# Output projection of a hybrid encoder layer: four full products per 512 columns, or seven quarter products per 1024 columns with weight sums made by accumulating transfers

## The chip, the cores and the metric

One core of one Trainium2 chip runs the kernel. The metric is the device time of one execution in microseconds; several executions give a median. The engines are TensorE (PE; its weight loads are shown as PEld), VectorE (DVE), ScalarE (ACT), GpSimd (POOL) and SyncE (SP, which here only issues transfers). Sixteen DMA engines move data between DRAM and SBUF. The profile is one execution recorded by the hardware profiler.

## The reference

One layer over 16 meta tokens and 512 frames of width 2048, in float32. Only the end touches the change: `mix` (tokens x 2048) times `w_out` (2048 x 2048), added to the residual, then a final RMSNorm.

```python
hn = _rmsnorm(h_res, norm_in_g[l])
P = hn @ w_in[l]
...
y_a = (yn + bonus.reshape(bsz, L, D_RWKV)) * jax.nn.silu(g_r)
...
y_b = Bg * _causal_depthwise_conv(Cg * hc, conv_w[l]) * jax.nn.silu(g_c)
mix = jnp.concatenate([y_a, y_b], axis=-1)
h_res = h_res + mix @ w_out[l]
...
out = _rmsnorm(h_res, norm_f_g)
return out[:, N_META:]
```

## The kernel before

The kernel has two large matrix products and a recurrence between them. The input product (`steps`, L315) runs 65 column tiles of `w_in` through TensorE; it is a generator, and `fill` draws matmuls from it to put between the small matmuls of the recurrence (`recur`). TensorE's order is written by hand. On the other engines a scheduler sets the order, by what it expects to be ready; each engine then runs strictly in that order and waits at its next instruction. `ahead()` and `high_priority` move instructions forward in it.

Every float32 operand of a large product is split in two parts: `hi`, a rounded copy made by ACT, and `lo`, the rest, made by a subtraction on VectorE or POOL. A product is then three matmuls: hi x hi, hi x lo, lo x hi. `split_w` (L123) does it for a 128x512 quarter of weights; `hi` and `lo` have six buffers each. `prefetch` (L130) loads 128x1024 blocks (512 KB) through SP into three `raw` buffers and splits them. SP, too, runs in order: a load waits there until the `raw` buffer that it writes has been split.

`split_mix` (L1022) makes the left operand of the output product: for each of 16 tiles `j` of 128 mix columns (8 of the recurrence, 8 of the convolution) it loads the tile from DRAM, applies group-norm gain, bonus and gate where `j < 8`, and splits it. The last convolution tile (`cv7`) is written to DRAM (`mixd`) after the last input product and read back.

The output product (L1151 and following) goes over four blocks `n` of 512 output columns, 16 tiles `jj` of the contraction and four tiles `t` of 128 tokens; `accumulate` (L1080) issues the three matmuls. Each block uses four PSUM banks. `residual` (L1091) adds the bank to the residual rows `xr`, and takes the squares on ACT and the gain on POOL. The last block is split: its last six tiles `jj` run token tile by token tile (`load_last`, `last`), and the last token tile in two parts of 256 columns, so that norm, scaling and stores of the other rows (`finish`) overlap the rest. `row_part`, `row_scale` and `finish_last` make the norm of the last row and its four stores.

Of the kernel before, what the change touches and what calls it, by code (L numbers as in the profile page):

```python
# [76 lines left out]
def hymba_kernel(ctx: ExitStack, tc: tile.TileContext, xt, xtok, w_in, w_out, pv, lup, cst, msk, gf, out):  # L77
# [39 lines left out]
    for n in range(4):  # L117
        for g in range(8):
            stream.append(w_out[n, g])
# [897 lines left out]

    pp = ctx.enter_context(tc.tile_pool(name="pp", bufs=1, side="right", reuse_waits="tile"))
    order = list(range(KT))
    parts = {}  # L1020

    def split_mix(j):  # L1022
        parts[j] = [pp.tile([P, SEQ], F32R, name=f"m{a}{j}") for a in range(2)]
        mh, ml = parts[j]
        raw = pp.tile([P, SEQ], F32, tag="mraw", name=f"mr{j}", bufs=4)
        if j < NPAIR:
            rb = pp.tile([P, SEQ], F32, tag="rb", name=f"rb{j}", bufs=3)
            gg = pp.tile([P, SEQ], F32, tag="gg", name=f"gg{j}", bufs=3)
# [12 lines left out]
        nc.scalar.copy(mh, raw)  # L1041
        nc.vector.tensor_tensor(out=ml, in0=raw, in1=mh.bitcast(F32), op=ALU.subtract)
# [5 lines left out]
    for j in range(NPAIR):  # L1048
        split_mix(j)
        fill(FW["mix"])  # L1050
    for j in range(NPAIR + 4, KT):
        while ("gc", j - NPAIR) not in ready:
            step()
        run_pending(float("inf"))
        split_mix(j)
    for _ in flow:
        pass
    ph1.close()
# [4 lines left out]
    xr = [pw.tile([P, DM], F32, name=f"xres{t}") for t in range(4)]  # L1063
    gfb = pw.tile([P, DM], F32, name="gfb")
    ssq = pw.tile([P, 4, 5], F32, name="ssq")
    fv = pw.tile([P, 4, 3], F32, name="fv")
    NL = 6
    last = [[pw.tile([P, 512], F32R, name=f"wlast{a}{j}") for j in range(NL)] for a in range(2)]

    def load_last(jj):  # L1070
        j = N_IN + 3 * 8 + jj // 2
        if jj % 2 == 0:
            state["raw"] = wp.tile([P, 1024], F32, tag="raw", name=f"wr{j}", bufs=3)
            nc.sync.dma_start(state["raw"], stream[j])
        rq = state["raw"][:, (jj % 2) * 512 : (jj % 2 + 1) * 512]
        hi, lo = last[0][jj - (KT - NL)], last[1][jj - (KT - NL)]
        nc.scalar.copy(hi, rq)
        nc.vector.tensor_tensor(out=lo, in0=rq, in1=hi.bitcast(F32), op=ALU.subtract)

    def accumulate(ps, t, jj, hi, lo, parts_of=range(2)):  # L1080
        mh, ml = parts[order[jj]]
        tk = slice(t * P, (t + 1) * P)
        for q, (mm, ww) in enumerate(((mh, hi), (mh, lo), (ml, hi))):
            whole = len(ps) == 4 or t < 3
            for p in (0,) if whole else parts_of:
                o = slice(0, 512) if whole else slice(256 * p, 256 * p + 256)
                nc.tensor.matmul(  # L1087
                    ps[t + p], mm[:, tk], ww[:, o], start=(jj == 0 and q == 0), stop=(jj == KT - 1 and q == 2)
                )

    def residual(ps, n, t, part=None):  # L1091
        o = slice(0, 512) if part is None else slice(256 * part, 256 * part + 256)
        h = xr[t][:, n * 512 : (n + 1) * 512][:, o]
        nc.vector.tensor_tensor(out=h, in0=ps[t + (part or 0)], in1=h, op=ALU.add)
        sq = pw.tile([P, 512], F32, tag="sqj", name=f"sqj{n}_{t}_{part}", bufs=2)
        j = n + (part or 0)
        nc.scalar.activation(sq[:, o], h, AF.Square, scale=DM**-0.5, accum_out=ssq[:, t, j : j + 1])
        if n < 3:
            nc.gpsimd.tensor_tensor(out=h, in0=h, in1=gfb[:, n * 512 : (n + 1) * 512], op=ALU.mult)
        elif part is not None:  # L1100
            nc.vector.tensor_tensor(out=h, in0=h, in1=gfb[:, n * 512 : (n + 1) * 512][:, o], op=ALU.mult)

    scales = {}
# [6 lines left out]

    def row_scale(t, n):
        f = fv[:, t]
        w, u, r = f[:, 0:1], f[:, 1:2], f[:, 2:3]
        nc.gpsimd.tensor_scalar(out=u, in0=ssq[:, t, n : n + 1], scalar1=w, scalar2=None, op0=ALU.add)
        rsqrt(r, u)
        scales[t] = r

    def finish(t):
        r = scales[t]
        x = xr[t]  # L1120
        o = out[t * P : (t + 1) * P]
        nc.vector.scalar_tensor_tensor(
            out=x[:, 1536:DM], in0=x[:, 1536:DM], scalar=r, in1=gfb[:, 1536:DM], op0=ALU.mult, op1=ALU.mult
        )
        nc.gpsimd.tensor_scalar(
            out=x[:, 1024:1536], in0=x[:, 1024:1536], scalar1=r, scalar2=1.0, op0=ALU.mult, op1=ALU.mult
        )
        nc.scalar.activation(x[:, 0:1024], x[:, 0:1024], AF.Copy, scale=r)
        for a, b in ((1024, DM), (0, 1024)):
            nc.sync.dma_start(o[:, a:b], x[:, a:b])  # L1130

    def finish_last(t):
        r = scales[t]
        x = xr[t]
        o = out[t * P : (t + 1) * P]
        nc.vector.tensor_scalar(
            out=x[:, 1536:DM], in0=x[:, 1536:DM], scalar1=r, scalar2=1.0, op0=ALU.mult, op1=ALU.mult
        )
        nc.sync.dma_start(o[:, 1536:DM], x[:, 1536:DM])
        nc.scalar.activation(x[:, 0:512], x[:, 0:512], AF.Copy, scale=r)  # L1140
        nc.scalar.dma_start(o[:, 0:512], x[:, 0:512])
        nc.gpsimd.tensor_scalar(
            out=x[:, 1024:1536], in0=x[:, 1024:1536], scalar1=r, scalar2=1.0, op0=ALU.mult, op1=ALU.mult
        )
        nc.vector.tensor_scalar(
            out=x[:, 512:1024], in0=x[:, 512:1024], scalar1=r, scalar2=1.0, op0=ALU.mult, op1=ALU.mult
        )
        nc.sync.dma_start(o[:, 512:1024], x[:, 512:1024])
        nc.scalar.dma_start(o[:, 1024:1536], x[:, 1024:1536])

    for n in range(4):  # L1151

        ps = [
            po.tile([P, 512 if n < 3 or t < 3 else 256], F32, tag="o", name=f"o{n}_{t}") for t in range(4 if n < 3 else 5)
        ]
        first = KT if n < 3 else KT - NL
        for jj in range(first):
            idx = N_IN + n * 8 + jj // 2
            if jj % 2 == 0:
                prefetch(min(idx + 2, len(stream) - NL // 2))  # L1160
            if n < 2 and jj % 4 == 2:
                t, cols = jj // 4, slice(0, 512) if n == 0 else slice(512, DM)
                nc.sync.dma_start(xr[t][:, cols], xtok[t * P : (t + 1) * P, cols])
            if n == 0 and jj == KT - 1:
                nc.sync.dma_start(gfb, gf.partition_broadcast(P))
            if n == 3 and jj >= first - NL:
                load_last(jj + NL)
            hi, lo = quarters[2 * idx + jj % 2]
            for t in range(4):
                accumulate(ps, t, jj, hi, lo)  # L1170
        if n < 3:
            for t in range(4):
                residual(ps, n, t)
    with tc.manual_schedule(engines={mybir.EngineType.DVE, mybir.EngineType.Activation, mybir.EngineType.Pool}):
        for t in range(3):
# [4 lines left out]
            if t:  # L1180
                finish(t - 1)
# [70 lines left out]
```

## Time and profile before

| what | us |
|---|---|
| median of 3 runs (1049.66 to 1050.91) | 1050.04 |
| the profiled run | 1049.89 |
| span of the profiled execution | 1048.1 |
| mean granted TensorE clock | 0.996 of full |

The work of the last stage, in windows of the same execution (busy us of each engine in 20 us):

| window, us | PE | DVE | ACT | POOL | DMA share | GB/s |
|---|---|---|---|---|---|---|
| 870 to 890 | 20.00 | 3.34 | 4.97 | 4.42 | 0.82 | 300 |
| 890 to 910 | 20.00 | 5.35 | 6.81 | 7.85 | 0.28 | 79 |
| 910 to 930 | 20.00 | 2.08 | 4.35 | 7.39 | 0.35 | 106 |
| 970 to 990 | 20.00 | 2.77 | 4.69 | 3.88 | 0.36 | 106 |
| 990 to 1010 | 20.00 | 9.68 | 8.98 | 9.82 | 0.35 | 106 |

Busy time is the time in which an engine had an instruction running; a matmul's record overlaps the next one's, so a full PE column says that TensorE never waited, not that it was at its peak. The DMA share is the mean busy share of the 16 DMA engines. "Wait" and "releaser" in the profile are inferred from semaphores.

### The profile page before, as it was taken

How to read it: one execution, taken by the hardware profiler on the slowest of the kernel's cores; microseconds unless marked ns; L12 is line 12 of the kernel's file. 1: busy time of each engine (PE TensorE's matmuls, PEld its weight loads, DVE VectorE, ACT ScalarE, POOL GpSimd, SP SyncE). 2: the span in 40 equal slices, each digit the busy share in tenths (PEclk: the TensorE clock that was granted, in tenths of full speed). 3: DMA queues.
4: the chain of work that ended last, by engine and by line, in shares of the span. 5: the costliest groups of instructions: out<-in, count | busy, mean ns of one | idle time of the engine just before them, and what ended most of it. 6: DMA issues, size and time to landing. Idle time of an engine off the chain costs nothing.

```text
span 1048.1 us, 23743 instructions
## 1 busy us (share of the span) xinstructions
PE 1030.6 (98%) x9845; PEld 940.2 (90%) x9845; DVE 577.1 (55%) x1088; ACT 359.7 (34%) x666; POOL 302.2 (29%) x315
## 2 busy tenths in 40 slices
PE   8999999999999999999999999999999999999996
PEld 6999997999988999989999989889898988888885
DVE  6787865569653768643767642344554781212222
ACT  7554322534322433222433222222222432323232
POOL 0132323323232322222323221233323132424132
PEclk9999999999999999999999999999999999999998
DMA  8437385374854274754374748677655978332324
GB/s 292 142 103 175 84 215 143 99 176 102 213 143 118 84 187 105 182 157 116 104 171 115 186 127 291 232 222 241 186 152 137 270 214 304 101 87 94 101 61 161
DMA packets 183404, 167.48 MB, mean 160 GB/s; under 512 B 121472, under 2 KB 143744, under 8 KB 182912
## 3 DMA queue, kind: packets, MB, share of 16 engines
q1 hardware_dynamic: 182720, 164.90, 55.6%
q8 instruction: 77, 1.26, 0.5%
q10 hardware_dynamic: 576, 1.07, 0.3%
q14 instruction: 31, 0.25, 0.1%
HBM read 129.05 MB, written 36.88 MB: 158 GB/s over the span
## 4 chain that ended last, share of the span: by engine, by line
PE 92%; DMA 4%; DVE 2%; SPq 1%; issue 1%; ACT 0%; POOL 0%; DVEq 0%; ACTq 0%
PE o L1087 17%; PE ps_v L315 9%; PE ps_gc L315 9%; PE ps_k L315 9%; PE ps_g L315 9%; PE ps_r L315 8%; PE ps_B L315 8%; PE ps_C L315 7%; PE ps_h L315 7%; PE g L631 2%; PE zs L954 1%; PE ps_lora L315 1%; PE zy L958 1%; DMA gated<-g 1%; PE rz L902 1%; DVE wl L127 1%
## 5 line engine op out<-in xcount | busy, mean ns | idle before, releaser
L127 POOL TENSOR_TENSOR wl<-wr,wh 128x512 fp32r<-128x512 f32 x150 | 204.4, 1363 | 466.0 <-ACT wh L126 450.4
L126 ACT CAST wh<-wr 128x512 fp32r<-128x512 f32 x312 | 189.7, 618 | 407.1 <-PE o L1087 93.9
L127 DVE TENSOR_TENSOR wl<-wr,wh 128x512 fp32r<-128x512 f32 x162 | 122.2, 761 | 205.9 <-ACT wh L126 204.7
L1087 PE MATMUL o<-wh,m 128*128 128x512 f32 (+1 forms) x484 | 145.4, 384 | 0.0
L1087 PEld LDWEIGHTS o<-wh,m 128*128 128x128 f32 x484 | 89.6, 188 | 21.3
L1087 PE MATMUL o<-wl,m 128*128 128x512 f32 (+1 forms) x242 | 92.7, 390 | 0.0
L315 PE MATMUL ps_v<-xh,wh 128*128 128x264 f32 x256 | 73.2, 286 | 0.0
L315 PE MATMUL ps_h<-xh,wh 128*128 128x258 f32 (+1 forms) x256 | 73.0, 285 | 0.0
L315 PE MATMUL ps_k<-xh,wl 128*128 128x264 f32 x256 | 73.0, 285 | 0.0
L315 PE MATMUL ps_k<-xh,wh 128*128 128x264 f32 x256 | 73.0, 285 | 0.0
L315 PE MATMUL ps_v<-xh,wl 128*128 128x264 f32 x256 | 72.8, 284 | 0.0
L315 PE MATMUL ps_v<-xl,wh 128*128 128x264 f32 x256 | 72.8, 284 | 0.0
L315 PE MATMUL ps_k<-xl,wh 128*128 128x264 f32 x256 | 72.7, 284 | 0.0
L315 PE MATMUL ps_C<-xh,wh 128*128 128x258 f32 (+1 forms) x256 | 72.7, 284 | 0.0
L315 PE MATMUL ps_r<-xh,wh 128*128 128x258 f32 (+1 forms) x256 | 72.3, 282 | 0.3 <-ACT wh L225 0.3
L315 PE MATMUL ps_g<-xl,wh 128*128 128x258 f32 (+1 forms) x256 | 72.5, 283 | 0.0
L315 PE MATMUL ps_h<-xl,wh 128*128 128x258 f32 (+1 forms) x256 | 72.1, 281 | 0.3 <-issue 0.3
L315 PE MATMUL ps_h<-xh,wl 128*128 128x258 f32 (+1 forms) x256 | 72.3, 282 | 0.0
L315 PE MATMUL ps_r<-xh,wl 128*128 128x258 f32 (+1 forms) x256 | 72.1, 282 | 0.0
L315 PE MATMUL ps_r<-xl,wh 128*128 128x258 f32 (+1 forms) x256 | 72.1, 282 | 0.0
L315 PE MATMUL ps_C<-xl,wh 128*128 128x258 f32 (+1 forms) x256 | 72.1, 282 | 0.0
L315 PE MATMUL ps_g<-xh,wh 128*128 128x258 f32 (+1 forms) x256 | 72.1, 281 | 0.0
(274 smaller groups left out, 2705.2 us busy)
## 6 DMA issues: line engine op xcount, KB each, us to landing
wr<-in_w_in_dram SPq DMA_DIRECT2D x127, 512.0 KB
ct<-opd SPq DMA_DIRECT2D x64, 288.0 KB
wr<-in_w_out_dram SPq DMA_DIRECT2D x32, 512.0 KB
opd<-ar SPq DMA_DIRECT2D x8, 576.0 KB
opd<-gt SPq DMA_DIRECT2D x16, 288.0 KB
opd<-bt SPq DMA_DIRECT2D x64, 64.0 KB
xres<-in_xtok_dram SPq DMA_DIRECT2D x4, 768.0 KB
out_dram<-xres SPq DMA_DIRECT2D x6, 512.0 KB
```

Source lines behind the costliest of these rows:

```text
L126: nc.scalar.copy(hi, rq)
L127: eng.tensor_tensor(out=lo, in0=rq, in1=hi.bitcast(F32), op=ALU.subtract)
L315: nc.tensor.matmul(ps[r], ww[:, w], xx[:, kt, a:b], start=(kt == 0 and n == 0), stop=(kt == KT - 1 and n == 2))
L631: nc.tensor.matmul(z[h][:, c - c0], bk[hs, c, h : h + 2, :].rearrange("p a s -> p (a s)"), ar[hs, c].rearrange("p a s -> p (a s)"), start= ...
L902: nc.tensor.matmul(z[e][ho if e else hs, 0, k], t[hs, o : o + CH], t[hs, O_V : O_V + CH] if part else st[hs, 4 * e + k], start=(part == 0 ...
L954: nc.tensor.matmul(d[hs, j], w, x[hs], start=(a == 0), stop=(a == b - 1))
L958: nc.tensor.matmul(d[ho, j], t[hs, o : o + CH], x[hs], start=(a == 0), stop=(a == b - 1))
L1087: nc.tensor.matmul(ps[t + p], mm[:, tk], ww[:, o], start=(jj == 0 and q == 0), stop=(jj == KT - 1 and q == 2))
```

## The change

The input side stays as it is. The output product is done for 1024 output columns at a time ("half"). For each half the matrices are cut in quarters, `A` (tokens x contraction) by token half and contraction half, `B` (contraction x columns) likewise, and the four quarters of the result come from seven products of quarters (Strassen's method in Winograd's form) in place of eight. A product is four "units" `g`; a unit is one 512 KB block of weights, two tiles of the contraction, two tiles of tokens, twelve matmuls. The order of products is M1, M2, M7, Q6, P5, P4, M3.

The left sums (`S3`, `S5`, `S1`, `S4`) are made by VectorE in place in `mix` (`sums`), and split into hi and lo by `split_form`. The right sums are made by transfers: SP loads a block of `B`, then POOL issues a transfer that adds another block to it in SBUF (`add`); for Q6 and P4 the block of the product before is added to again (`chain`). Each unit is split two units ahead (`split_unit`), now always with the subtraction on VectorE. `close` combines a finished product into the residual rows `here(t, n)` and a shared sum. The table `calls` says at which unit each load, add and split is written in the program; the scheduler orders the engines but TensorE as before. The weights of the last product of the second half are loaded and split early (`load_home`) into buffers of forms no longer used. Rows are finished in the order 2, 3, 0, 1.

```diff
-    for n in range(4):
-        for g in range(8):
-            stream.append(w_out[n, g])
+    stream += [w_out[0, g] for g in range(2)]
...
+    mix = [pp.tile([P, 4, SEQ], F32, tag=f"R{m}", name=f"mix{m}") for m in range(4)]
...
-        nc.scalar.copy(mh, raw)
-        nc.vector.tensor_tensor(out=ml, in0=raw, in1=mh.bitcast(F32), op=ALU.subtract)
+        nc.scalar.copy(mh, raw[:, 0:n])
+        nc.vector.tensor_tensor(out=ml, in0=raw[:, 0:n], in1=mh.bitcast(F32), op=ALU.subtract)
...
+    forms = {"S3": (0, T1), "S5": (0, T0), "S1": (2, T1), "S4": (2, T0)}
+    def quarter(k, tk, q):
+        return mix[2 * k + q][:, :, tk]
+    def sums(q):
+        a11, a21, a12, a22 = quarter(0, T0, q), quarter(0, T1, q), quarter(1, T0, q), quarter(1, T1, q)
+        nc.vector.tensor_tensor(out=a22, in0=a22, in1=a21, op=ALU.subtract)
+        nc.vector.tensor_tensor(out=a21, in0=a11, in1=a21, op=ALU.subtract)
+        nc.vector.scalar_tensor_tensor(out=a11, in0=a22, scalar=-1.0, in1=a11, op0=ALU.mult, op1=ALU.subtract)
+        nc.vector.scalar_tensor_tensor(out=a12, in0=a11, scalar=-1.0, in1=a12, op0=ALU.mult, op1=ALU.subtract)
...
+    sums(0)
...
+    sums(1)
...
+    def split_form(f, q):
+        k, tk = forms[f]
+        x = mix[k + q][:, :, tk]
+        hi, lo = sform[f, q]
+        nc.scalar.copy(hi, x)
+        nc.vector.tensor_tensor(out=lo, in0=x, in1=hi.bitcast(F32), op=ALU.subtract)
+    PRODUCTS = ("M1", "M2", "M7", "Q6", "P5", "P4", "M3")
+    LEFT = {"M1": 0, "M2": T0, "M7": "S3", "Q6": "S5", "P5": "S1", "P4": T1, "M3": "S4"}
+    units = [(half, prod, g) for half in range(2) for prod in PRODUCTS for g in range(4)]
...
+    def request(u):
+        half, prod, g = units[u]
+        if prod in ("M1", "M2", "M3"):
+            k, c = {"M1": (0, 0), "M2": (1, 0), "M3": (1, 1)}[prod]
+        elif prod == "M7":
+            slot[u] = chain[g] = pw.tile([P, 1024], F32, tag=f"X{g}", name=f"x{half}{g}")
+            nc.sync.dma_start(slot[u], rows_of(half, 0, 1, g))
+            return
+        elif prod == "P5":
+            k, c = 0, 0
+            if g < 2:
+                slot[u] = spare[0][:, 1024 * g : 1024 * g + 1024]
+                nc.sync.dma_start(slot[u], rows_of(half, k, c, g))
+                return
+        else:
+            slot[u] = chain[g]
+            return
+        slot[u] = wp.tile([P, 1024], F32, tag="raw", name=f"wo{u}", bufs=3)
+        nc.sync.dma_start(slot[u], rows_of(half, k, c, g))
+    ADDED = {"M7": (1, 1), "Q6": (0, 0), "P5": (0, 1), "P4": (1, 0)}
+    def add(u):
+        half, prod, g = units[u]
+        if prod in ADDED:
+            k, c = ADDED[prod]
+            nc.gpsimd.dma_start(slot[u], rows_of(half, k, c, g), accum_op=ALU.add)
+    def split_unit(u, home=None):
+        for q in range(2):
+            rq = slot[u][:, q * 512 : (q + 1) * 512]
+            if home is None:
+                hi = wp.tile([P, 512], F32R, tag="hi", name=f"oh{u}{q}", bufs=6)
+                lo = wp.tile([P, 512], F32R, tag="lo", name=f"ol{u}{q}", bufs=6)
+            else:
+                hi, lo = home[q]
+            nc.scalar.copy(hi, rq)
+            nc.vector.tensor_tensor(out=lo, in0=rq, in1=hi.bitcast(F32), op=ALU.subtract)
+            right[u, q] = (hi, lo)
...
+    def product(u, bank, s_):
+        half, prod, g = units[u]
+        for s in s_:
+            for q in range(2):
+                jj = 2 * g + q
+                hi, lo = right[u, q]
+                for n, (m, w) in enumerate(((0, hi), (0, lo), (1, hi))):
+                    nc.tensor.matmul(
+                        bank[s], left(prod, jj, m, s), w, start=(jj == 0 and n == 0), stop=(jj == 7 and n == 2)
+                    )
+    def close(half, prod, z):
+        n = 2 * half
+        if prod == "M1":
+            shared[:] = [pw.tile([P, 512], F32, tag=f"sh{s}", name=f"sh{half}{s}") for s in range(2)]
+        for s in range(2):
+            d, p = shared[s], z[s]
+            if prod == "M1":
+                nc.scalar.copy(d, p)
+                onto(s, n, p, ALU.add)
+            elif prod == "M2":
+                onto(s, n, p, ALU.add)
+                squares(s, n)
+            elif prod == "M7":
+                onto(2 + s, n + 1, p, ALU.subtract)
+                onto(2 + s, n, p, ALU.add)
+            elif prod == "Q6":
+                with ahead():
+                    nc.vector.tensor_tensor(out=d, in0=d, in1=p, op=ALU.add)
+                nc.gpsimd.tensor_tensor(out=here(2 + s, n), in0=here(2 + s, n), in1=d, op=ALU.add)
+            elif prod == "P5":
+                with ahead():
+                    nc.vector.tensor_tensor(out=d, in0=d, in1=p, op=ALU.add)
+                for t in (2 + s, s):
+                    nc.gpsimd.tensor_tensor(out=here(t, n + 1), in0=here(t, n + 1), in1=d, op=ALU.subtract)
+                squares(2 + s, n + 1)
+            elif prod == "P4":
+                onto(2 + s, n, p, ALU.add)
+                squares(2 + s, n)
+            else:
+                onto(s, n + 1, p, ALU.subtract)
+                squares(s, n + 1)
...
+        if u >= N_FIRST:
+            early = {"M7": 7, "P5": 5}.get(prod, 3)
+            at(u - early, request, u)
+            at(u - (4 if prod == "M7" else 3), add, u)
+            at(u - 2, split_unit, u)
+    for f, (prod, off) in {"S3": ("M1", 0), "S5": ("M2", 0), "S1": ("M7", 0), "S4": ("Q6", 0)}.items():
+        for q in range(2):
+            at(U[0, prod] + off + 2 * q, split_form, f, q)
+    for t in range(4):
+        at((-1, 0, 3, 4)[t], load_xa, t)
+    at(U[0, "M7"] + 1, load_spare)
+    at(U[0, "P5"] + 1, lambda: globals_.update(gfb=load_gain()))
+    for m in range(2):
+        at(U[0, "P4"] + 2 + m, load_xb, m)
...
+    def load_home(g):
+        u = U[1, "M3"] + g
+        request(u)
+        tiles = [
+            pw.tile([P, 4, HT], F32R, tag=f"{f}{g % 2}{a}", name=f"home{g}{a}").rearrange("p a b -> p (a b)")
+            for f in (("S3", "S5")[g // 2],) for a in range(2)
+        ]
+        split_unit(u, [(tiles[0][:, 512 * q : 512 * q + 512], tiles[1][:, 512 * q : 512 * q + 512]) for q in range(2)])
+    for g in range(4):
+        at(U[1, "P5"] + 1 + 2 * g, load_home, g)
...
+        first = U[1, "M3"]
+        z = [po.tile([P, 512], F32, tag="o", name="end")]
+        for g in range(4):
+            product(first + g, z, (0,))
+        for t in (2, 3):
             row_part(t, 3)
...
             row_scale(t, 3)
...
+        finish(2)
+        row_part(0, 3)
+        row_part(1, 3)
+        h = here(0, 3)
+        nc.vector.tensor_tensor(out=h, in0=h, in1=z[0], op=ALU.subtract)
+        squares(0, 3)
+        row_scale(0, 3)
+        finish(3)
+        ends = [po.tile([P, 256], F32, tag="o", name=f"end{part}") for part in range(2)]
         for part in range(2):
...
+            cols = slice(256 * part, 256 * part + 256)
+            for jj in range(8):
+                hi, lo = right[first + jj // 2, jj % 2]
+                for n, (m, w) in enumerate(((0, hi), (0, lo), (1, hi))):
+                    nc.tensor.matmul(
+                        ends[part], left("M3", jj, m, 1), w[:, cols], start=(jj == 0 and n == 0), stop=(jj == 7 and n == 2)
+                    )
+            h = here(1, 3)[:, cols]
+            nc.vector.tensor_tensor(out=h, in0=h, in1=ends[part], op=ALU.subtract)
+            squares(1, 3, part)
+            gain(1, 3, nc.vector, cols)
             if part == 0:
...
+                finish(0)
+                nc.vector.tensor_tensor(out=fv[:, 1, 0:1], in0=fv[:, 1, 0:1], in1=ssq[:, 1, 3:4], op=ALU.add)
+        row_scale(1, 4)
+        finish_last(1)
```

More of the change, by code (lines that the diff above doesn't have):

```diff
@@ L1057, in hymba_kernel @@
         pass
+    sums(1)
+    pt.close()
     ph1.close()
@@ L1080, in accumulate @@
[L1080 to L1089, printed above, removed]
@@ L1139, in finish_last @@
[L1139 to L1148, printed above, removed]
@@ L1149, in finish_last @@
[L1149 to L1173, printed above, removed]
```

161 lines of the change are left out of this document (104 added, 57 removed).

## Prediction

> **What bounds the kernel now.** I read the busy table of the page first, then the chain of waits that ended last, cut to its end, then the groups of instructions of the last stage, and last the windows that show TensorE's clock and the transfer rate.
>
> ```profile
> PE 1030.6 (98%) x9845; PEld 940.2 (90%) x9845; DVE 577.1 (55%) x1088; ACT 359.7 (34%) x666; POOL 302.2 (29%) x315
> ```
>
> ```profile
> 849.78 10.89 PE ps_gc L315 x47
> 860.67 177.06 PE o L1087 x798
> 1037.73 0.02 issue
> 1037.75 0.44 DVE xres L1094
> ...
> 1042.73 0.84 DVEq L1248
> ```
>
> TensorE is busy for 98% of the span. In the chain's end the projection (L1087) runs from 860.67 for 177.06 us without a break, directly behind the last input product (L315): nothing else is on the path there. A removed matmul is therefore worth its whole period, as long as nothing else becomes late. After 1037.73 come the residual, norm and stores of the last row, 10.4 us to the end of the span (1048.1).
>
> The stage's groups, shapes kept apart (busy us, mean ns of one):
>
> ```profile
> L126 ACT CAST wh<-wr 128x512 fp32r<-128x512 f32 x52 | 32.2, 620 | 93.9 <-PE o L1087 93.9
> L1094 DVE TENSOR_TENSOR xres<-o,xres 128x512 f32<-128x512 f32 x15 | 9.5, 683 | 22.4 <-PE o L1087 22.4
> L1094 DVE TENSOR_TENSOR xres<-o,xres 128x256 f32<-128x256 f32 x2 | 0.8, 424 | 0.5 <-PE o L1087 0.5
> L1128 ACT ACTIVATE xres<-xres,fv 128x1024 f32<-128x1024 f32 x3 | 3.4, 1138 | 0.0
> ```
>
> ACT's splits wait 93.9 us in sum for TensorE to free a buffer: the helpers have room. The windows (busy us of PE, PEld, DVE, ACT, POOL with counts, then granted clock, DMA share, GB/s):
>
> ```profile
> 17.00:21.00 4.00, 2.05 (x9) 1.09 (x7) 3.90 (x7) 3.40 (x7) 0.00 (x0) 1.00 1.00 402
> 22.00:24.00 2.00, 2.00 (x9) 2.00 (x10) 1.90 (x4) 2.00 (x4) 0.00 (x0) 0.50 1.02 390
> 867.00:875.00 8.00, 8.00 (x36) 6.41 (x36) 1.44 (x2) 2.10 (x4) 2.59 (x2) 1.00 1.01 404
> 930.00:950.00 20.00, 20.00 (x87) 16.08 (x87) 3.90 (x7) 4.85 (x8) 3.88 (x3) 1.00 0.36 106
> ```
>
> Two things to see. All 16 DMA engines are full (share 1.01) at 404 GB/s, so a 512 KB load costs them 524288 / 404e3 = 1.30 us; in mid-stage they are a third used (0.36). And at the kernel's start, where TensorE was busy 2.05 of 4 us, its clock fell to 0.50 for the next 3.3 us or so: idle TensorE is paid twice.
>
> **The change part by part.** The measure is the profiled run, 1049.89 us, that is 1.8 us around its span of 1048.1; it lies 0.15 below the median of the runs, so terms are added to 1050.04.
>
> *Matmuls.* Before: 720 of 512 columns and 96 of 256, worth 768 widths of 512, in 177.06 us: 0.2306 us each (the 256 pairs cost the same within 0.02). The built order of the changed kernel has 648 of 512 and 48 of 256, worth 672. 96 x 0.2306 = **-22.1 us**. So the change does do what it says; that is no rival. A "unit" (12 matmuls on one 512 KB block, 56 of them) is 2.77 us; units 0 to 27 make the first half of the columns, seven products (M1, M2, M7, Q6, P5, P4, M3) of four units each.
>
> *Splits of weights and forms.* VectorE now makes every low part: 2 x 0.69 = 1.4 us per unit of 2.77. In the first half it also has 8 form splits and 4 sums over 1024 elements and 16 closing adds. No such 1024 row exists on VectorE; from 0.424 (256) and 0.683 (512), 1.20. 28 x 1.4 + 12 x 1.20 + 16 x 0.68 = 64 of 77.5 us; ACT 28 x 1.24 + 8 x 1.14 + 10 x 0.8 = 52. Hidden in the mean, 0; the cover is TensorE's own length. The four sums of the first columns (4.8 us) fall where VectorE was 34.5 of 50 us busy (800 to 850): 0, at most 4.8 were it full.
>
> *The seam at the sums.* The second set of sums needs the last convolution tile, which goes through DRAM (store at 863.9, load about 2.9 later), and VectorE's order puts them behind M1's closing add and in front of the split for unit 6: two adds, four sums, one form split, two splits = 2 x 0.68 + 5 x 1.20 + 2 x 0.69 = 8.7 us from the end of unit 3. TensorE holds work for units 4, 5 and a third of 6, 28 x 0.2306 = 6.5. Term **+2.3** (1 to 4, as ACT's turns fall). Queued behind are the splits of unit 7 and of M7.
>
> *The transfers.* This is where it turns. Before: 32 loads in the stage. Now 36 per half where 16 were: 20 loads and 16 adding transfers on POOL's queue. Nothing in this trace adds while it transfers. Low end 1.30 us of all engines (an add moves like a load); high end 3.9, three passes of 1.30 (fetch, read back, write, none beside another). I take **2.6**, two passes: the middle, and because the full row above is one read and one write per byte, and the add reads twice. I let POOL's transfers share the 16 engines, as ACT's queue does in the page's queue table. Now the first half. From 866.8, when SP is past the wait for the tile through DRAM, until unit 23 must have its block, 860.7 + 23 x 2.77 - 2 = 922.3, are 55.5 us. In that time SP issues, in its order, the mix tile (0.65 us), four xa, four x, wo7 (11.7), two spare, wo18, wo19 (5.2), the gain (2.6), wo24 (1.3), both xb (5.2), two spare again and wo25, wo26 (5.2): 31.9 us; with 16 adds of 2.6, 41.6, it is 73.5. Late by **+18**. With 1.30 it is 52.7, which just fits; with 3.9 it is 94.3, late by 38.8. The second half has 20 x 1.30 + 41.6 = 67.6 against 77.5 us: no wait.
>
> The Trainium skill, page "Collectives: The Full Stack", section "Part 3: Why 7× under link rate — side-by-side accounting", speaks against this change: a reducing transfer is slow not for its addition but for its two source reads on one ring, 32.35 GB/s against 62.28 for a copy. By that ratio, 1.93, an add would be 2.5 us and the term 16.5, an estimate; no run here shows it yet.
>
> *POOL's queue.* POOL issues in order, and behind the adds of P4 its order has the adds for the second half's first blocks before the close of P5 (L1212 of the changed kernel). The add of x10 waits for a load that waits for unit 20's split. ACT's squares of P5 wait for that close, and ACT's split of unit 23 stands behind the squares. On time, 0.68 + 1.3 + 0.8 + 0.6 + 0.7 = 4.1 us against 8.3 us of units 20 to 22: hidden. With transfers late it is not: x10 comes a load and an add (3.9) later. **+4** (0 to 6). An issue costs 0.33 us on SP; on POOL it is unknown, and below 2.6 it hides behind the transfer itself.
>
> *Clock.* TensorE would lack work for 18 of some 62 us in units 8 to 23, uneven. A loss like the one at 17 to 24.5 costs 3.3 x 0.5 = 1.65 us; 0 to 5 times; I take three, **+5**.
>
> *End.* The last 10.4 us keep their steps (256-wide add, square, power, four stores): 0, +-1.
>
> Sum: -22.1 + 2.3 + 18 + 4 + 5 = +7.2, **1057 us**.
>
> **The rivals.**
>
> *Adds as cheap as loads: faster.* One mechanism, the price of an add, decides the sign: with 2.3 + 4 + 5 kept, the stage breaks even when lateness is 10.8, i.e. (55.5 + 10.8 - 31.9) / 16 = 2.15 us per add. At 1.30 the lateness is 0, but the engines are 95% full, so single blocks come late; I give 4, the clock and POOL nothing: -22.1 + 2.3 + 4 = -15.8, **1034 us**. For it: mid-stage the engines are a third used, and the reading of SBUF may overlap. Against it: share 1.01 at 404 GB/s. The same time follows if POOL's transfers had engines of their own (41.6 and 31.9 are both under 55.5).
> The Trainium skill, page "DMA: Bandwidth & Descriptors", section "Issuing engines are not separate DMA queues", says that they do not: all queues run on the same 16 engines.
>
> *Adds at three passes: much slower.* Lateness 38.8, and the second half, 20 x 1.30 + 62.4 = 88.4 against 77.5, adds some 6; clock and POOL 10: -22.1 + 2.3 + 38.8 + 6 + 10 = +35, **1085 us**. For it: fetch and read-back of a short row may not overlap. Against: engines work on eight rows each.
>
> *Adds one at a time on POOL.* If each add must land before the next issues, with about 2 us beside its 2.6: 16 x 4.6 = 74 us from 872, where the first x lands, to 946, 24 late: -22.1 + 2.3 + 24 + 9 = +13, **1063 us**. Against: they write different tiles, and the built order makes none wait for the one before.
>
> **How the numbers follow.** Forecast 0.42 (own range 1046 to 1068), cheap adds 0.34, three passes 0.14, one at a time 0.10. The range leaves a tenth out on each side: 1032 to 1082, from the cheap case nearly to the dear one. A measurement of this kernel can tell about 0.2% (2.1 us). Slower by more: 0.42 x 0.9 + 0.14 + 0.10 = 0.61; within 0.2%: 0.05, out of the forecast's low edge and the cheap case's high one; faster 0.34.
>
> **What would show it.** Right: DMA share near 1.0 from 867 to about 930 and 0.8 after; TensorE's idle time put down to transfers into x, spare and wo (split by L1155), mostly in units 8 to 23; some windows at clock 0.5; the second half at 77.5 us. Seam: one wait of 2 to 3 us near 878. Wrong: adds landing in the time of loads and share well under 1 (cheap case), or waits for adds in the second half too (three passes). The forecast falls whole if lateness of the first half is under 11 us.

## The result, and the profile after

The changed kernel took 1066.71 us (median of four runs, 1064.62 to 1067.81) against 1050.1 us for the kernel before on the same chip: 1.0155 times as long, 95% interval 1.0136 to 1.0174. The direction of the forecast was right and the time lies inside its range, but the loss is 16.6 us where 7 was forecast. The profiled run took 1065.86 us, 15.97 more than that of before, with a span of 1064.1.

The page of the changed kernel: the busy table, then its two large DMA queues (packets, MB, share of 16 engines' span).

```profile
PE 1022.3 (96%) x9725; PEld 926.4 (87%) x9725; DVE 664.6 (62%) x1195; ACT 394.4 (37%) x726; POOL 313.2 (29%) x332
...
q1 hardware_dynamic: 184784, 169.09, 55.4%
q0 software_dynamic: 4608, 16.78, 8.1%
```

Queue q0 holds the 32 adds and nothing else. 8.1% of 1064.1 us over 32 is **2.69 us of all 16 engines for one add**; the prediction had bounded this by 1.30 and 3.9 and taken 2.6.

The end of the chain of waits of the changed kernel (start, us, what):

```profile
1013.15 7.28 DMA wo<-in_w_out_dram
1020.43 0.02 issue
1020.45 0.63 ACT home L1155
...
1023.60 2.78 DVE ol L1156 x2
1026.38 0.04 issue
1026.42 17.57 PE P L1184 x68
1043.99 5.48 PE end L1184 x24
1049.47 5.76 PE end L1368 x48
...
1058.08 0.84 DVEq L1433
```

The last matmul ends at 1055.23, so 8.9 us follow it. The projection ran from 860.65, for 194.58 us. Before it was 179.2 us, from 860.67 to 1039.87, with 8.2 us behind it: the 177.06 us in the chain of before hold only 798 of its 816 matmuls, because that chain leaves TensorE at 1037.73. The other 18 come after it. Windows of the kernel before, TensorE's busy time first behind the length:

```profile
1038.00:1039.00 1.00, 1.00 (x11) 1.00 (x10) 0.36 (x2) 0.88 (x4) 0.85 (x2) 1.00 0.97 397
1039.00:1040.00 1.00, 0.87 (x8) 0.67 (x6) 1.00 (x4) 0.83 (x1) 0.00 (x0) 1.00 1.02 422
```

The last stall of the changed kernel is in the second half, at 1022.9 to 1026.4, behind a load that took 7.28 us.

TensorE's waits in the stage (855 to 1064; us in total, times, longest):

```profile
PE P L1184 <- DVE ol L1156: 12.9, 5, 5.8
PE Q L1184 <- ACT oh L1155: 5.6, 2, 5.3
PE M L1184 <- DVE ol L1156: 4.1, 6, 3.0
PE P L1184 <- ACT oh L1155: 0.5, 1, 0.5
PE Q L1184 <- DVE ol L1156: 0.2, 1, 0.2
```

They are 23.3 us together. Windows of 3.4 us on the grid on which the clock changes (busy us of PE, PEld, DVE, ACT, POOL with counts, then granted clock, DMA share, GB/s):

```profile
906.70:910.10 3.40, 0.00 (x0) 0.00 (x0) 0.00 (x0) 0.00 (x0) 0.88 (x1) 1.00 1.06 277
910.10:913.50 3.40, 2.13 (x4) 1.45 (x5) 2.15 (x3) 1.14 (x2) 0.87 (x1) 0.50 1.06 252
913.50:917.00 3.50, 3.50 (x10) 2.68 (x9) 3.50 (x7) 1.14 (x2) 0.88 (x1) 0.51 1.05 260
917.00:920.40 3.40, 3.40 (x16) 2.77 (x15) 2.88 (x5) 2.19 (x4) 0.89 (x1) 1.00 1.08 250
...
1022.80:1026.20 3.40, 1.06 (x4) 0.48 (x3) 3.40 (x4) 0.87 (x2) 3.02 (x2) 1.00 0.51 154
1026.20:1029.60 3.40, 3.18 (x8) 2.50 (x9) 3.40 (x7) 2.80 (x5) 0.00 (x0) 0.50 0.00 0
```

A stretch in which TensorE mostly waits is followed by one at clock 0.50: TensorE is busy throughout 913.50 to 917.00, yet completes 10 matmuls there where the next stretch has 16. Eight such stretches lie in the stage (882.8, two from 910.1, 944.3, three from 951.1, 1026.2). TensorE was busy for 20.9 us in them, so half of that, 10.5 us, is what they add in this account; whether they cost it is what `warm` asks. The DMA share is 1.0 or more in the first four rows, as it is from 870 to 960.

Where the 194.58 us lie by place: a unit that nothing disturbs takes 2.80 us here (0.2333 a matmul). The table gives, for each kernel's profiled run, the time from a unit's first matmul to the next unit's, less 2.80 (us); the kernels are told below. In warm the extra matmuls, 14.5 us, count as lost. The last column is half the time at clock 0.50, idle time included.

| kernel | 0-5 | 6-7 | 8-15 | 16-19 | 20-23 | 24-27 | 28-43 | 44-51 | sum | clock |
|---|---|---|---|---|---|---|---|---|---|---|
| changed | 0.0 | 4.8 | 12.3 | 0.0 | 15.6 | 0.4 | 0.0 | 4.5 | 37.6 | 13.7 |
| no_adds | 0.0 | 3.8 | 0.0 | 0.0 | 0.2 | 0.0 | 0.0 | 0.0 | 4.0 | 1.7 |
| copies | 0.0 | 5.5 | 2.3 | 0.0 | 3.2 | 0.0 | 0.0 | 0.0 | 11.1 | 1.7 |
| pool_order | 0.0 | 2.9 | 8.7 | 10.5 | 9.1 | 0.0 | 6.7 | 17.3 | 55.1 | 15.4 |
| close_dve | 0.0 | 4.0 | 12.3 | 0.0 | 2.5 | 9.1 | 1.1 | 6.6 | 35.5 | 12.0 |
| sp_late | 7.5 | 3.9 | 6.2 | 0.0 | 0.0 | 0.0 | 10.5 | 6.9 | 35.0 | 13.6 |
| sums_late | 0.0 | 5.5 | 13.7 | 3.6 | 9.6 | 0.0 | 0.0 | 6.1 | 38.4 | 10.2 |
| combo1 | 6.8 | 5.6 | 4.6 | 0.0 | 0.0 | 0.0 | 8.2 | 7.1 | 32.3 | 8.5 |
| ring2 | 0.0 | 3.1 | 13.5 | 0.0 | 17.0 | 0.0 | 1.1 | 8.0 | 42.7 | 13.7 |
| home_late | 0.0 | 4.1 | 12.2 | 0.0 | 16.6 | 0.0 | 0.6 | 2.5 | 36.2 | 12.0 |
| home_act | 0.0 | 5.9 | 10.9 | 0.0 | 17.5 | 0.3 | 0.0 | 0.0 | 34.6 | 13.7 |
| no_sums1 | 0.0 | 4.2 | 11.3 | 0.0 | 16.2 | 0.0 | 0.0 | 2.6 | 34.3 | 10.2 |
| warm | 2.3 | 0.8 | 15.5 | 0.0 | 13.6 | 0.0 | 0.1 | 2.4 | 34.6 | 5.1 |

So for the changed kernel: 648 x 0.2333 + 48 x 0.120 (the chain's last row, 5.76 / 48) = 157.0 us of matmuls, 22.2 under 179.2; 37.6 lost; 0.6 more at the end: -22.2 + 37.6 + 0.6 = 16.0. Of the 37.6, 23.3 are waits, 10.5 the clock, and the rest, 3.8, delays that the view of waits does not list (units 8 to 11 lose 3.4, of which it lists 1.1).

### The profile page after: what moved, and what is told of

Same layout as the page of the kernel before. It is cut to its first block, busy times and chain, and to the rows that moved or that the text cites. A ratio compares the mean times of both kernels' runs of the same rounds, so it can differ in the third digit from the quotient of the medians.

```text
span 1064.1 us, 23777 instructions
## 1 busy us (share of the span) xinstructions
PE 1022.3 (96%) x9725; PEld 926.4 (87%) x9725; DVE 664.6 (62%) x1195; ACT 394.4 (37%) x726; POOL 313.2 (29%) x332
## 5 line engine op out<-in xcount | busy, mean ns | idle before, releaser
L125 POOL TENSOR_TENSOR wl<-wr,wh 128x512 fp32r<-128x512 f32 x123 | 171.1, 1391 | 377.0 <-ACT wh L124 354.2
L124 ACT CAST wh<-wr 128x512 fp32r<-128x512 f32 x258 | 156.3, 618 | 311.5 <-PE ps_k L313 52.0
L125 DVE TENSOR_TENSOR wl<-wr,wh 128x512 fp32r<-128x512 f32 x135 | 100.6, 752 | 100.5 <-ACT wh L124 100.0
L313 PE MATMUL ps_g<-xh,wl 128*128 128x258 f32 (+1 forms) x256 | 71.9, 281 | 0.0
L313 PE MATMUL ps_C<-xh,wl 128*128 128x258 f32 (+1 forms) x256 | 71.9, 281 | 0.0
L1156 DVE TENSOR_TENSOR ol<-x,oh 128x512 fp32r<-128x512 f32 x48 | 43.2, 928 | 31.0 <-ACT oh L1155 30.8
```

What stands on the lines that cost most here:

```text
L125: eng.tensor_tensor(out=lo, in0=rq, in1=hi.bitcast(F32), op=ALU.subtract)
L313: nc.tensor.matmul(ps[r], ww[:, w], xx[:, kt, a:b], start=(kt == 0 and n == 0), stop=(kt == KT - 1 and n == 2))
```

## The experiments

All are edits of the changed kernel. The start of the stage shifts by up to 2.6 us from run to run (858.1 to 860.6 in the profiled runs), so a gain of that size is read from the table, not from the medians.

**What an add costs.** `copies`:

```diff
-            nc.gpsimd.dma_start(slot[u], rows_of(half, k, c, g), accum_op=ALU.add)
+            nc.gpsimd.dma_start(slot[u], rows_of(half, k, c, g))
```

> Leaves out the sums of weights: each adding transfer is a plain copy of the same 512 KB on the same queue of POOL into the same tile, so only the price of the addition is gone. Theory A (as predicted: the DMA engines are full because an add costs them 2.6 to 2.7 us): with 1.30 us each the first half asks 31.9 + 16 x 1.30 = 52.7 us of 55.5, so the waits of units 8 to 23 (28.5 us with the clock) go but for some 3, and that of unit 46 (4.6) too: 1034 to 1040 us. Theory B (order in the queues: POOL's close of Q6 and P5 stands behind an add for the second half, ACT's split of a home block in front of unit 46): the 15 us of units 22 and 23 stay: 1048 to 1054 us.

Measured: 1040.69 us (1037.80 to 1042.99), 0.9912 of before [0.9888, 0.9937]. Its queue of the same 32 transfers:

```profile
q0 software_dynamic: 4608, 16.78, 4.4%
```

4.4% of a span of 1036.0 us over 32 is 1.42 us for a copy where an add costs 2.69. The adding alone is 26.0 us of the 1066.71, and units 20 to 23 (3.2 us left) and 46 recover although POOL's and ACT's orders are unchanged. Theory A: the median lies 0.7 us above its range, the profiled run (1037.80) inside it. Up to seven of the copies were in flight at a time, where it was three of the adds; `ring2` below shows what that alone is worth.

`no_adds` leaves the transfers out:

```diff
-        if prod in ADDED:
-            k, c = ADDED[prod]
-            nc.gpsimd.dma_start(slot[u], rows_of(half, k, c, g), accum_op=ALU.add)
+        return
```

> Leaves out the sums of weights and their transfers altogether: every product takes one loaded block. What is left beside the matmuls saved is the seam at the second set of sums and the unit's own period. A and B alike: -22.1 + 4.9 (seam) + 1.6 (56 units at 2.80 in place of 2.77 us) - 1.5 (end) on 1050 = 1033, range 1031 to 1036. Theory C (VectorE and ACT bound the stage, 64 and 52 of 77.5 us by the prediction's count, in bursts): waits for the low parts stay without any add: 1040 or more.

Measured: 1031.01 us (1030.79 to 1031.68). This is what both theories expected. All transfers of the adds together cost 35.7 us. Without adds VectorE and ACT hide all of their splits and forms; only the seam stays (3.8).

**POOL's queue.** In the changed kernel three waits hang together (waits of POOL, DVE and ACT, 872 to 962):

```profile
POOL spare L1145 <- DMA spare<-in_w_out_dram: 6.6, 1, 6.6
...
DVE sh L1210 <- POOL xa L1207: 6.5, 1, 6.5
...
ACT sqj_None L1171 <- POOL xa L1212: 11.0, 2, 9.8
```

An add for the second half waits for its load, the close of Q6 stands behind it, VectorE's add for P5 behind that, and ACT's squares, with the split of unit 23 behind them, wait for the close of P5. `pool_order` holds POOL to the written order, in which the closes come first:

```diff
+    order_ = ExitStack()
+    order_.enter_context(tc.manual_schedule(engines={mybir.EngineType.Pool}))
     for fn, args in calls.pop(-1):
...
+    order_.close()
```

> The same work; only POOL's instructions of the stage keep the order in which they are written, so that the closes of Q6 and P5 stand in front of the adds of the second half. Theory B: units 22 and 23 lose their 15 us: 1051 to 1054 us. Theory A: the blocks of units 22 and 23 land at 937 and 941 whatever stands in the queue, and at most 4 us go: 1062 to 1066 us.

Measured: 1082.78 us (1081.02 to 1084.56), 16 slower. Both theories missed. POOL's waits of that kernel (900 to 1062):

```profile
POOL xa L1207 <- DVE sh L1206: 9.6, 2, 8.1
...
POOL xa L1212 <- DVE sh L1210: 6.4, 1, 6.4
```

TensorE's largest row there (855 to 1078):

```profile
PE P L1184 <- ACT oh L1155: 22.5, 4, 6.4
```

Now the adds stand behind closes that wait for TensorE's product: units 18, 22, 46 and 50 each lose 7 us or so. Neither order of the one queue serves both. `close_dve` takes the closes away from it:

```diff
-                nc.gpsimd.tensor_tensor(out=here(2 + s, n), in0=here(2 + s, n), in1=d, op=ALU.add)
+                nc.vector.tensor_tensor(out=here(2 + s, n), in0=here(2 + s, n), in1=d, op=ALU.add)
...
-                    nc.gpsimd.tensor_tensor(out=here(t, n + 1), in0=here(t, n + 1), in1=d, op=ALU.subtract)
+                    nc.vector.tensor_tensor(out=here(t, n + 1), in0=here(t, n + 1), in1=d, op=ALU.subtract)
```

> The closes of Q6 and P5 (6 adds of 128x512 a half) run on VectorE in place of POOL, whose queue then holds adding transfers and gains alone; the same transfers. In the changed kernel units 22 and 23 lost 15.0 us, and POOL stood 6.6 us at an add for the second half with the close behind it; keeping the written order was no cure (1082.8 us), since the adds then stand behind a close that waits for TensorE. Theory B (one queue for both): the 15 us go but for 3: 1052 to 1056 us, VectorE's 4 us more a half hidden. Theory A (engines full, the blocks of units 22 and 23 land at 937 and 941 all the same): 1061 to 1065 us.

Measured: 1060.85 us (1059.13 to 1066.00). TensorE's waits there from 930 to 975:

```profile
PE M L1184 <- ACT oh L1155: 6.9, 1, 6.9
PE P L1184 <- DVE ol L1156: 1.9, 2, 1.1
```

Units 20 to 23 fall from 15.6 to 2.5 us, as theory B had it, although their last blocks land when theory A said (934.76 and 938.60, in a stage that began 2.6 us earlier). But the loss moves on to M3's last block, unit 27: its load was issued at 941.86, behind loads for the second half, and landed at 958.66. Units 24 to 27 rise from 0.4 to 9.1. So the head of POOL's queue decided which unit paid, and by itself it is worth 15.6 + 0.4 - 2.5 - 9.1 = 4.4 us of the first half. In time that is theory A, 0.15 us below its range.

**Whether the first half is overfull.** `sp_late` holds SP to the written order and writes the second half's loads later:

```diff
-    at(U[0, "P5"] + 1, lambda: globals_.update(gfb=load_gain()))
+    at(U[0, "M3"] + 2, lambda: globals_.update(gfb=load_gain()))
...
-        at(U[0, "P4"] + 2 + m, load_xb, m)
+        at(U[1, "M1"] + m, load_xb, m)
...
+    order_ = ExitStack()
+    order_.enter_context(tc.manual_schedule(engines={mybir.EngineType.SP}))
...
+    order_.close()
```

> SP keeps the written order of the stage's loads, and xb and the gain are written at units 28, 29 and 26, so that both xb (5.2 us of all engines), the gain (2.6) and the second half's spare pair (2.6) leave the first half: 73.5 - 10.4 = 63.1 us of transfers for 55.5, late by 7.6 in place of 18. Theory A: units 8 to 23 lose some 12 us in place of 28.5: 1048 to 1053 us if the second half (67.6 + 10.4 = 78 of 77.5 us) loses no more than now. Theory D (POOL's queue holds three adds at a time, and their own landing, 9.4 us in the median, sets the pace whatever else is loaded): 1062 or more.

Measured: 1062.13 us (1060.78 to 1063.49). In time this is where theory D put it, and theory A missed by 9 us; `ring2` below tests D by itself. Units 8 to 27 fall from 28.3 to 6.2, more than theory A asked, but the second half rises from 4.5 to 17.4, and units 0 to 5 lose 7.5 that the written order itself causes (SP's waits, 855 to 880):

```profile
SPq L418 <- DVE cv L417: 13.5, 1, 13.5
```

A load of w_out stands there behind the store of the last convolution tile, which waits for VectorE. So most of the first half's loss goes when transfers leave it, and comes back where adds fill the engines too. How much of the fall is due to the moved loads is open, as the 7.5 us lost ahead of these units also gave their transfers more time.

`sums_late` writes the second sums behind the split of unit 6:

```diff
-    sums(1)
     pt.close()
...
+    at(5, sums, 1)
+    for f, (prod, off, late) in {"S3": ("M1", 0, 4), "S5": ("M2", 0, 2), "S1": ("M7", 0, 0), "S4": ("Q6", 0, 0)}.items():
...
-            at(U[0, prod] + off + 2 * q, split_form, f, q)
+            at(U[0, prod] + off + 2 * q + late * q, split_form, f, q)
```

> The second set of sums stands behind the split of unit 6, and the two form splits that need it later by as much. The seam (units 6 and 7, 4.9 us in the changed kernel, 3.9 without adds) goes: 1061 to 1064 us. Rival: VectorE has no room there and the wait moves to units 7 to 11: 1065 to 1068.

Measured: 1064.53 us (1060.76 to 1067.24); units 6 and 7 still lose 5.5 (4.8 in the changed kernel). The wait now stands in front of unit 7: ACT's form splits wait for the sums, and the split of unit 7 stands behind them. That is the rival's place, though the median lies between the two ranges. `no_sums1` leaves these sums out altogether:

```diff
-    sums(1)
     pt.close()
```

> Leaves out the second set of the four sums (the tokens' quarters with the later half of the features), which stands on VectorE in front of the split of unit 6. The prediction's seam: 8.7 us of VectorE against 6.5 of cover; without the four sums (4.9 us at 1.22 each) 3.8 against 6.5: no wait at units 6 and 7, and the stretch of half clock behind it (1.7 us) goes with it. 4.5 to 5 us less: 1061 to 1063 us. Rival: the full engines make the block of unit 6 or 7 late by as much, 1065 to 1068.

Measured: 1063.55 us (1060.73 to 1066.90); units 6 and 7 still lose 4.2. The median lies between the two ranges again. The seam has two causes of about one length: without the adds the sums alone give 3.8, and with the sums gone ACT waits 2.9 us for unit 7's block, whose load stands behind xa and x at a DMA share of 1.0.

`combo1` joins close_dve, sp_late, sums_late and home_late:

> close_dve, sp_late, sums_late and the home blocks of home_late together. What stays is an add's price: 63.1 us of transfers for 55.5 in the first half, 78 for 77.5 in the second. On the 1031 us without adds: + 7.6, a clock loss of 1.7 to 3.4, a wait or two in the second half of 0 to 5, less 4 for the seam: 1037 to 1044 us, faster than before. Rival: the full engines make single blocks late in both halves, 1048 to 1058.

Measured: 1059.53 us (1058.45 to 1060.83), 1.0095 of before [1.0080, 1.0110]. The rival, 1.5 us above its range: units 8 to 27 lose only 4.6, but 15.3 come back in the second half and 6.8 at the start. In none of these orders did 32 adds cost less than they save; the loss was moved.

**How many adds in flight.** `ring2`:

```diff
-    nc = _bacc.Bacc("TRN2", target_bir_lowering=False, num_devices=1, dynamic_dma_scratch_size=1024)
+    nc = _bacc.Bacc("TRN2", target_bir_lowering=False, num_devices=1, dynamic_dma_scratch_size=2048)
```

> The store for the descriptors of POOL's transfers is 2048 bytes in place of 1024, nothing else. In the changed kernel POOL issues three adds, and then each next one 0.25 to 0.3 us after the third before it has landed (886.62 to 886.87, 890.23 to 890.49, 894.10 to 894.36). Theory D (three in flight set the pace of the adds): six in flight take a larger share of the full engines, the adds land earlier, and units 12 to 23 lose some 10 us less: 1054 to 1060 us. Theory A (the engines are full, and who gets them changes little): 1064 to 1068; the landing of one add then takes about twice as long.

Measured: 1066.12 us (1064.73 to 1070.02). POOL issues earlier and up to seven adds are in flight, not three, but each takes longer (KB, median us from issue to landing; 9.4 in the changed kernel):

```profile
x<-in_w_out_dram POOLq DMA_DIRECT2D x24, 512.0 KB, 10.9
```

The last add of the first half landed 64.9 us after the first was issued (874.95 to 939.88), in place of 63.8 (877.04 to 940.89). Theory A in time, and the pace is not set by the three in flight; its other sign, a landing about twice as long, did not come in the median.

**The clock.** `warm`:

```diff
+    WARM = {(0, 6): 10, (0, 12): 18, (0, 22): 14, (0, 23): 20}
...
+        if (half, u) in WARM:
+            pz = po.tile([P, 512], F32, tag="o", name=f"warm{u}")
+            for i in range(WARM[half, u]):
+                nc.tensor.matmul(pz, left("M1", 0, 0, 0), right[u - 1, 1][0], start=True, stop=True)
         product(u, z, range(2))
```

> Matmuls whose result is not used (10, 18, 14 and 20 of 512 columns, 2.3, 4.2, 3.3 and 4.7 us) stand in front of units 6, 12, 22 and 23, where TensorE waited 3.0, 5.3, 4.1 and 6.4 us, so that the waits are no longer idle. In the changed kernel the clock was 0.50 in eight stretches of 3.41 us, 13.65 us lost. Theory E (that loss is paid in full): some 8 of the 11.5 us of these units go: 1057 to 1061 us. Theory A (the blocks come at the pace of the full engines, and time that the slow clock takes would be waited for anyway): 1064 to 1069 us.

Measured: 1061.59 us (1059.71 to 1066.72), 5.1 less, between the two ranges. Three stretches of the stage stay at half clock, not eight (3.6 us by the count above, not 10.5). But the table gives little of the gain to the matmuls added: units 0 to 27 lose 32.2 us in place of 33.1. Another 2.1 us is unit 46, where none was added, and the stage began 1.8 us earlier. After the extra matmuls TensorE still waited 4.9 us in unit 13 and 2.8 in unit 23, so they were not what made it late. Where they stood, 5.3 us less of half clock came out as 0.9 us of time in the profiled runs. By place that is theory A: the blocks come at the pace of the full engines, and a TensorE that stays at full clock waits longer for them.

**Unit 46.** `home_late` writes the loads of the last product's blocks later:

```diff
-        at(U[1, "P5"] + 1 + 2 * g, load_home, g)
+        at(U[1, "P4"] + g, load_home, g)
```

> The four blocks kept for the last product are loaded and split from unit 48 on, one a unit, in place of units 45, 47, 49 and 51 as written. Theory B: ACT's split of such a block in front of unit 46 waits for its load (5.5 us) and makes TensorE wait; with the load later the 4.6 us of unit 46 go: 1062 us, 1061 to 1063.5. Theory A2 (the adds of the second half fill the engines, and the block of unit 46 itself is late): no change, 1065 to 1068.

Measured: 1063.83 us (1061.66 to 1065.95). Undecided: 4.5 became 2.5, and ACT's built order still had a home block in front of unit 46. `home_act` makes sure of it:

```diff
-        request(u)
...
-        at(U[1, "P5"] + 1 + 2 * g, load_home, g)
+        at(U[1, "P4"] - 1 + g, request, U[1, "M3"] + g)
+        at(min(U[1, "P4"] + 1 + g, U[1, "P4"] + 3), load_home, g)
...
+        if u == U[1, "P5"]:
+            order_ = ExitStack()
+            order_.enter_context(tc.manual_schedule(engines={mybir.EngineType.Activation}))
...
+    order_.close()
```

> The changed kernel, with the splits of the home blocks on ACT held behind the splits of units 49 to 51 (ACT keeps the written order from unit 44 on), and their loads at units 47 to 50. In home_late ACT's queue still had the third home block in front of unit 46, and unit 46 still lost 2.6 us. Theory B (the home block in front of unit 46): units 43 to 47 lose nothing: 4.6 us less, 1061 to 1063 us. Theory A2 (full engines make unit 46's own block late, or the loss returns at units 48 to 55): 1065 to 1068.

Measured: 1062.19 us (1060.79 to 1063.46), and units 44 to 51 lose nothing at all. Theory B: unit 46's own block had landed at 995; its split stood on ACT behind that of a block that came late. That block was late because of the adds (in copies, with the old order, nothing is lost there).

**Seven products where there is room.** `half2` computes columns 0 to 1023 by plain products and uses the method for columns 1024 to 2047 alone, with six of the 16 adds written early:

```diff
+    EARLY = {"M7": lambda u, g: (24 + 2 * g, 27 + 2 * g), "P5": lambda u, g: (28 + 2 * g, 31 + 2 * g) if g < 2 else (u - 5, u - 3)}
...
+    for b in range(N_FIRST, 16):
+        at(2 * b - 4, request_block, b)
+        at(2 * b - 3, split_unit, ("b", b))
+    for q in range(2):
+        at(2 * q, split_a21, q)
+        at(4 + 2 * q, sums, q)
```

> Eight plain products for columns 0 to 1023 (as before, in 512 KB blocks of 24 matmuls), seven products for columns 1024 to 2047 alone; the adds of M7 and of P5's first two blocks are issued while the plain half runs, and the sums and forms are made under it. 720 widths of 512 in place of 768: -11.1 us. 16 adds of 2.69 and some 46 loads of 1.30 are 103 of 166 us. Theory A (full engines were what cost): no seam, no late blocks in the plain half, 0 to 5 us in the second half: -11.1 + 0.9 (28 units at 2.80) - 1.5 + 0 to 5: 1038 to 1044 us, faster than before. Rival F (each add is late by its own landing and by the queues, full engines or not): the second half's waits stay or grow, 1046 to 1055.

Measured: 1042.63 us (1040.79 to 1045.72), 0.9941 of before [0.9921, 0.9961]. TensorE waits 2.0 us in the whole stage, at the third unit of P5. `half2b` adds the edit of home_act:

> half2 with the edit of home_act. half2 waited 2.0 us in all, at the third unit of P5, for a low part. Theory B: that goes: 2 us under half2 (1042.6), 1039 to 1042 us and 0.7 to 1.1 per cent under before. Theory A2: as half2, 1042 to 1044.

Measured: **1039.45 us (1039.06 to 1040.15), 0.9909 of before [0.9895, 0.9924]**. Its stage in two windows (the plain half, then the seven products; columns as above):

```profile
859.60:949.20 89.60, 89.60 (x386) 72.08 (x385) 47.94 (x59) 34.91 (x57) 13.14 (x12) 1.00 0.75 229
949.20:1027.70 78.50, 78.48 (x361) 64.16 (x359) 54.98 (x81) 41.09 (x77) 30.24 (x32) 1.00 0.59 142
```

TensorE is busy without a break at full clock, and the DMA share is 0.75 and 0.59, not 1.0. Half the matmuls saved, and nothing lost: 9.7 us faster than the kernel before on the same chip, and 27 under the changed kernel's 1066.71. These kernels have half the adds and also more time for them; no run separates the two.

## Why the prediction was off

*Matmuls, -22.1.* Found -22.2 (179.2 to 157.0). The step misread the chain of before: it divided 177.06 us, the time of 798 matmuls, by the widths of all 816, 0.2306 each, and let the last row begin at 1037.73. Matmuls of 512 columns take 0.2333 in the changed kernel and those of 256 take 0.120. With 0.2333 the term is -22.4, so the slip hardly shows.

*Splits and forms, 0.* Right without adds: the stage then loses 4.0 us, 3.8 of them at the seam. Not right beside them: TensorE's 5.8 us at unit 23 are a wait for one subtraction of VectorE that took 6.30 us in place of 0.68 (last section). The prediction has no such term.

*The add, 2.6.* Right: 2.69, and 1.89 times a copy on the same queue (1.42). The Trainium skill, page "Collectives: The Full Stack", section "Part 3: Why 7× under link rate — side-by-side accounting", which puts this down to two source reads, gave 1.93; the trace agrees with the ratio, and no run here shows its cause.

*Transfers +18, POOL's queue +4, clock +5 in units 8 to 23: 27.* Found 28.3 (12.3 + 15.6 + 0.4). The cause was right: the last block that was to be there at 922.3 landed at 940.89, 18.6 late, POOL's queue alone was 4.4 by close_dve, and with the cheaper transfers of copies, in the same orders, 5.5 of the 28.3 are left. The nearness of the sum is in part luck. The 28.3 are 17.7 of waits where 22 were forecast, 7.2 of half clock where it was 5, and 3.4 of short delays where it was nothing, and 5.8 of the waits are the subtraction that the prediction did not know.

*The clock is the term that was mis-sized.* "A loss like the one at 17 to 24.5 costs 3.3 x 0.5 = 1.65 us; 0 to 5 times; I take three, +5." In the account of the time it came eight times, for 10.5 us: six times in units 8 to 24, and once each at units 6 and 46, to which the step gave none. Every wait of 3 us or more drew one or more, and so did the two of 1.8 and 0.7 us at unit 46. The total of the waits, 2.3 + 18 + 4 = 24.3 us against 23.3, came out by chance: fewer in units 8 to 23, and 2.5 at unit 46 that were not forecast. Nor does the step's way of adding the clock to the lateness hold: in warm 5.3 us less of half clock gave 0.9 back.

*Seam, 2.3.* The wait was 3.0, inside its bounds; 1.7 of half clock behind it make up most of the 4.8. Its one named cause, VectorE's 8.7 us, was half of the truth: unit 7's load is late by about as much.

*"The second half has 20 x 1.30 + 41.6 = 67.6 against 77.5 us: no wait."* This step failed outright: TensorE lost 4.5 us at unit 46 where it was to lose nothing, and home_act, which takes away what stood in front of that unit, loses nothing in units 44 to 51. A mean over the half hid that 10 adds and four loads fall into 985 to 1021, some 32 of 36 us, and that an in-order engine hands one late block on to a block that is there.

*End, 0.* Found +0.6 (8.23 to 8.87), inside its +-1. By place the misses sum to -0.1 + 2.5 + 1.3 + 4.5 + 0.6 = 8.8, and 7.2 + 8.8 = 16.0: the loss was more than twice the forecast because the second half waited and the seam cost twice its term. By kind they are 5.5 of half clock and 3.8 of short delays, against 1.0 less of waits; -0.1 and 0.6 are the rest.

*Rivals.* Cheap adds (1034) fell with the price, and copies shows what they would have given. Three passes (1085): the price excludes it. One at a time (1063) came nearest in time, but not by its mechanism: three were in flight, and twice the room for them changed nothing.

*What was to show it.* DMA share 1.0 "from 867 to about 930" lasted to 960; the idle time was in units 8 to 23 but for 5.6 us; the seam's wait and the half clock were seen. The second half did not keep to its 77.5 us; a wait there was to point to three passes, but the price was two.

## What to carry to other kernels

Work saved on the engine that bounds a kernel is paid for elsewhere: count what it asks of the DMA engines in the stretch where they are already full, not over the whole stage. A method that trades matmuls for transfers pays where the transfers can be spread; here half of it gave 10 us and all of it lost 17 (16.6). Where TensorE will wait, expect half clock after each wait of a few us, but do not add it to a lateness of transfers as a term of its own: what the clock gives back may be waited for. Put instructions that wait on different things on different in-order queues.

## What the runs showed of the hardware

POOL has three adds in flight with 1024 bytes of store for descriptors: it issues the next 0.25 to 0.3 us after the third before it has landed (886.62 to 886.87, 890.23 to 890.49). With 2048 bytes up to seven are in flight, and of the plain copies up to seven with 1024. An issue takes it 0.88 us for an add, and 0.56 for a plain copy.

VectorE seems to be shut out while POOL works without a break. Timelines of the changed kernel from 948.8 to 956.0, VectorE first, then POOL (start, us; its spans are rough):

```profile
949.34 6.90 DVE L1156 TENSOR_TENSOR ol<-x,oh 128x512 fp32r<-128x512 f32 x2 [3.62 <-ACT oh L1155]
```

```profile
947.65 4.05 POOL L1212 TENSOR_TENSOR xa<-xa,sh 128x512 f32<-128x512 f32 x3
951.33 1.23 POOL L1145 DMA_DIRECT2D x<-in_w_out_dram  x1
951.95 3.12 POOL L1175 TENSOR_TENSOR xa<-xa,gfb 128x512 f32<-128x512 f32 x2
954.39 1.53 POOL L1145 DMA_DIRECT2D x<-in_w_out_dram  x1
```

Two subtractions of 0.68 us take 6.90, the first alone 6.30, with all inputs there at 949.30; TensorE's 5.8 us at unit 23 are this wait. It came again, 6.27 to 6.37 us long, in warm, ring2, home_act, home_late, sums_late and no_sums1. In copies the longest is 5.16, and in close_dve, where POOL has no closes, 3.56 (at 927.93, beside two of POOL's multiplications by the gain). In the changed kernel four such subtractions last over 2.2 us (6.30, 3.56, 2.64, 2.39), and each ends 0.55 to 0.57 us after the last of POOL's tensor operations beside it, and the longest while a transfer issue of POOL still ran. No run takes POOL's work away alone, so the cause is argued from this timing. The Trainium skill, page "SBUF — State Buffer", section "🔬 SBUF: two separate sides", tells of a port pair that VectorE and POOL hold exclusively, for a whole instruction; the trace agrees in kind, but the wait here spans several instructions of POOL.

What stays open: how much of the 4.4 us of POOL's queue is this wait and how much the order, and what makes up the short delays of 3.8 us.
